# Two gates' weights and the second convolution product split anew in every chunk instead of reloaded from a scratch copy

## The chip, the cores and the metric

The kernel runs on one core of one Trainium2 chip. The metric is the device time of one execution in microseconds (us). Of the kernel before, three executions took 1346.3, 1350.51 and 1344.78 us, the median being 1346.3 us. A profile was taken of one further execution, of which all rows below are.

## What is computed

One layer over 2048 tokens of width 1024, with 16 learned meta tokens put ahead of them:

```
u = rms_norm(h, pre_norm_g)
glu_a, glu_b, conv_gate, q, k, v, sb_gate = split(u @ w_in)        # 7 x 512 columns
c = layer_norm(causal_depthwise_conv(glu_a * sigmoid(glu_b)))      # width 31
c = (silu(c) @ w_pw2 + b_pw2) * silu(conv_gate)
s = stick_breaking_attention(q, k, v) * silu(sb_gate)              # 8 heads of 64
h = h + rms_norm(concat(c, s) @ w_out, post_norm_g)
```

The attention is strictly causal; the weight of key s for query t is beta[t,s] times the product of (1 - beta) over the keys between them. Input and output are float32.

## The kernel before

**Chunks and streams.** The tokens are worked off in four chunks of 512 (`NCH`, `TC`). Chunk c has a main stream, `attention(c)`, and a fill stream, which is in this order the stick-breaking gate (`sb_gate`, weights `G_SG`), the output projection of chunk c-1 (`out_proj`, weights `w_out`), the convolution gate (`conv_gate`, weights `G_CG`), the second convolution product (`conv_out`, weights `w_pw2`) and the input projection of chunk c+1 (`in_proj`: GLU, keys, values, queries). Beside them run the convolution's taps (on DVE, or for some channel groups of chunks 2 and 3 on ACT and POOL as `conv_apart`), the layer norm of the convolution (`conv_norm`) and the split of its result into `mixs` (`conv_parts`). A small planner at build time (`Clock`, `Engine`, `merge`, `step`) keeps a model of each engine's time and writes all instructions out in one order; on the chip every engine then works its queue in that order, and an instruction that waits holds up all behind it. All instructions carry the line of the planner's `issue` helper, L206, so the rows are told apart by tile names.

**Products in three parts.** Each float32 operand is taken as a high part (rounded to float32r) and a low part (the rest), and each product is three matmuls: high by high, high by low, low by high. The two parts of a weight slab (128 partitions by 512 columns) come from `split` (line 442): ACT copies the slab into the high part, then POOL (DVE for seven early slabs) subtracts it from the slab and writes the low part.

**Where the weights come from.** `specs` (465) lists every use of every slab in order, with a turn: 0 for the input projection of chunk 0, and 1 + c for what chunk c's fill stream uses. There are 76 slabs: 56 of `w_in` (8 to each of the seven 512-column groups), 4 of `w_pw2`, 16 of `w_out`. A use goes one of two ways (`prepare`, 538):

- taken apart: two neighbouring slabs come in one 512 KB load from the input (`load_raw`, tile `wr`, named `wr<-wpack`), and `split` writes the parts into a `w` tile;
- kept: both parts, made earlier and stored by a DMA from POOL's queue (`keep_it`, `wscr<-w`, 512 KB a slab), come back with one 512 KB load a slab (`w<-wscr`, or `wr<-wscr`).

Turn 0 takes its slabs apart and stores nothing. From turn 1 on each slab is taken apart at its first use, stored, and kept from then on. So chunk 0's gates, `w_pw2` and the input projection of chunk 1 are taken apart and stored, chunk 1 still does that with `w_out`, and all else is kept.

**Slots.** There are four `w` tiles (`WB`) and two `wr` tiles (`RAWS`). While raw pairs are still to come the `wr` tiles hold them, two pairs ahead; once no raw pair is left they serve kept slabs as well, so that six slabs can be under way:

```
if tags.count("w") < WB:
    tag, bufs = "w", WB
elif not (raws or todo_raw) and tags.count("wr") < RAWS:
    tag, bufs = "wr", RAWS
```

A product gives a slot back (`release`, 580) after the last matmul of a slab; `out_proj` holds the four slabs of a column group through its first half and gives them back one by one in the second.

**Marks.** A string among an action's outputs is a mark; `force(mark)` (268) makes the planner write out, there and then, all pending actions that bear it. The values of a chunk are made by `values` (935) for four groups of two heads: differences, transposes on PE (`turn`), split, and a store to DRAM (`vscr<-mixs`). All four groups bear the mark `"v"`. `load_v` (1203) forces it ahead of the first loads of a chunk's own values (`vk<-vscr`); so do `meta_v`, `meta_keys` and `tail`.

Of the kernel before, what the change touches and what calls it, by code (L numbers as in the profile page):

```python
# [19 lines left out]
P = 128  # L20
# [3 lines left out]
NM = 16  # L24
# [230 lines left out]
def trunk(ctx: ExitStack, tc: tile.TileContext, x, xturn, meta, cpack, post_g, wpack, out):  # L255
# [16 lines left out]
    def when(what, ins, outs=(), engine=None, date=0.0, tag=None):  # L272
        soon.append(Later(clock, what, ins, outs, engine, date, tag))
# [191 lines left out]
    def specs():  # L465
        def cols(g):
            for j in range(NJ):
                yield w_in, (g + j) * P, P, 0, KD

        def proj_specs(c):  # L470
            for j in range(NJ):
                yield w_in, (G_B + j) * P, P, 0, KD
                yield w_in, (G_A + j) * P, P, 0, KD
            yield from cols(G_K)
            yield from cols(G_V)
            yield from cols(G_Q)

        def out_specs(k0, k1):
            for n in range(0, D, OC):
                yield w_out, n, OC, k0, k1  # L480

        def chunk(c):
            yield from cols(G_SG)
            if c > 0:
                yield from out_specs(0, KD)
            yield from cols(G_CG)
            for j in range(NJ):
                yield w_pw2, j * P, P, 0, NJ
            if c + 1 < NCH:
                yield from proj_specs(c + 1)  # L490
            else:

                for n in (*range(0, D, OC), *range(D // 2, D, OC)):
                    yield w_out, n, OC, 0, KD - 1

        for spec in proj_specs(0):
            yield 0, spec
        for c in range(NCH):
            for spec in chunk(c):
                yield 1 + c, spec  # L500
# [9 lines left out]
    place = {key: wscr[i] for i, key in enumerate(again)}  # L510
    order = []
    there = set()
    for turn, (w, n0, cols, ka, kb) in specs():
        step_k = 4 * P // cols
        for k0 in range(ka, kb, step_k):
            key = w, n0, cols, k0
            n = (min(k0 + step_k, kb) - k0) * cols
            kept, save = key in there, key not in there and key in place and turn > 0
            if save:
                there.add(key)  # L520
            order.append((key, n, kept, save))
# [413 lines left out]
    def values(c):  # L935

        for j in range(NJ):
            vts = []  # L940

            def ev_v(pt, o, n):
                if not vts:
                    vt = T("ev", [P, 1 + NM + TC], EV)
                    vts.append(vt)
                    if c == 0:
                        pool.memset(vt[:, 0:1], 0.0)
                    else:
                        pool.tensor_copy(
                            vt[:, NM : NM + 1], vcol[(c - 1) % 2][:, j, NTB - 1 :]  # L950
                        )
                act.activation(vts[0][:, 1 + o : 1 + o + n], pt, AF.Copy)

            yield from proj(c, G_V + j, ev_v, True)

            def differences(vt, j):
                o = 0 if c == 0 else NM
                dv = T("ev", [P, 1 + NM + TC], EV)[:, : NM + TC]
                pool.tensor_tensor(
                    dv[:, o:], vt[:, o : NM + TC], vt[:, o + 1 :], op=ALU.subtract  # L960
                )
                pool.tensor_copy(vcol[c % 2][:, j], vt[:, NM + P :: P])
                when(lambda: turn(dv, j, P, NM, NTB), [dv], ["v"], tag="T")
                if c == 0:
                    when(lambda: turn(dv, j, NM, 0, 1), [dv], ["v"], tag="T")

            def turn(dv, j, rows, t0, nb):
                pt = PT("T", [P, NTB, P])[:rows, :nb]
                for b in range(nb):
                    pe.transpose(pt[:, b], dv[:, t0 + b * rows : t0 + (b + 1) * rows], ident)  # L970
                for b in range(0, nb, 2):
                    n = min(2, nb - b)
                    part = T("mixs", [P, 2, 4, HD], 8, F32R)[:rows, 0:n]
                    hi, lo = part[:, :, 0::3, :], part[:, :, 1:3, :]
                    d = pt[:, b : b + n].rearrange("p b (h d) -> p b h d", d=HD)
                    act.activation(hi, d, AF.Copy)
                    dve.tensor_tensor(lo, d, hi.bitcast(F32), op=ALU.subtract)
                    row = c * TC + t0 + b * rows
                    when(
                        lambda row=row, n=n, part=part: sp.dma_start(  # L980
                            vscr[j, row : row + n * rows, :].rearrange(
                                "(b p) d -> p b d", p=rows
                            ),
                            part.rearrange("p b k d -> p b (k d)").bitcast(F32),
                        ),
                        [part], ["v"],
                    )

            when(lambda vt=vts[0], j=j: differences(vt, j), [vts[0]], [vcol[c % 2], "v"])
            if c == 0 and j == 0:  # L990
                in_us(4.5, meta_k, outs=[km])

# [8 lines left out]
                )  # L1001

    def meta_v():
        force("v")
        for h in range(NH):
            e, j = h % 2, h // 2
            rows = slice(e * HD, (e + 1) * HD)
            for i in range(2):
                blk = (0 if i == 0 else 1) if e == 0 else (3 if i == 0 else 2)
                sp.dma_start(  # L1010
                    vm[h * NM : (h + 1) * NM, i, j, rows].bitcast(F32),
                    vscr[j, 0:NM, blk * HD : (blk + 1) * HD],
                )
# [186 lines left out]
    def attention(c, mixs):  # L1200
        heads = {}

        def load_v(h, kc):
            if kc == c:
                force("v")
            s0, e = NM + kc * TC, h % 2
            vk = T("vk", [P, NTB, P], 2, F32R)
            sp.dma_start(
                vk.bitcast(F32),
                vscr[h // 2, s0 : s0 + TC, e * P : (e + 1) * P].rearrange(  # L1210
                    "(b p) d -> p b d", p=P
                ),
            )
            return vk
# [208 lines left out]
    def meta_keys(c, h0, h1, mixs):  # L1423
# [4 lines left out]
            given=lambda: all(("total", c, h) in keep for h in range(h1))  # L1428
            and (c < NCH - 1 or ("conv", c) in keep)
        )  # L1430
        force("v")
        bm = ev()[:, :TC].rearrange("p (b h s) -> p b h s", b=NTB, h=NH)
        hold.add(bm.name)
        if part:
# [339 lines left out]
    def tail(c):  # L1774


        force("v")
        sw, gates = [], [T("mixc", [P, TC], 8) for _ in range(NJ)]
        one = [conv_gate(c, gates), conv_out(c, sw, gates, mixc[c])]
        two = [conv_parts(c, accs[c], sw)]  # L1780
        if c + 1 < NCH:
            one.append(in_proj(c + 1))
            two.append(turn_in(c + 1))
        else:
            one.insert(1, last_room(c))
        yield from either(chain(*one), chain(*two))
# [117 lines left out]
```

## Time and profile before

| | |
|---|---|
| median of three executions | 1346.3 us |
| the profiled execution, its own time | 1350.2 us |
| its span | 1348.5 us |
| PE busy | 1315.5 us, 98% |
| DVE busy | 1014.4 us, 75% |
| ACT busy | 723.5 us, 54% |
| POOL busy | 644.6 us, 48% |
| moved by DMA | 304.96 MB, mean 226 GB/s |
| granted PE clock over the span | 0.994 |

PE is the tensor engine and PEld its weight load, DVE the vector, ACT the scalar and POOL the GpSimd engine; SPq is the queue of SyncE, which issues most DMAs. "mm<-uh,w" reads: tile `mm` was written from tiles `uh` and `w`. Busy time of PE counts the pipelined ends of matmuls, so 98% doesn't mean that nothing is left; idle time in a short stretch is what shows a stall. "[7.88 <-DMA wr<-wpack]" behind an instruction says that its engine stood idle 7.88 us before it, and that the landing of that DMA ended the wait.

By the evacuations and stores in the trace the stages lie thus, in us from the span's start: input projection 0 to about 133; chunk 0's gates and `conv_out` to 218; input projection of chunk 1 to about 355; chunk 1's gates, output projection and `conv_out` to 500; input projection of chunk 2 to 664; the same two of chunk 2 to 830 and 1013; chunk 3's to 1250; then the end.

### The profile page before, as it was taken

What the parts mean: (1) busy time and instruction counts of PE and PEld (TensorE: products, weight loads), DVE (VectorE), ACT (ScalarE), POOL (GpSimd) and SP (SyncE); (2) the same over time, 40 slices, a digit from 0 to 9 for tenths busy, and PEclk for the clock granted to TensorE, in tenths of its full rate; (3) what the DMA queues carried; (4) which work ended last, traced back from release to release, by engine and by line L of the source; (5) the groups of instructions that cost most, each with busy time, mean ns of one, the idle gap of its engine ahead of it and who ended that gap; (6) DMA issues with size and microseconds to landing.
All of it is one profiled execution on the core that took longest, in us unless ns stands there. A gap on an engine that the chain in (4) does not pass through costs nothing.

```text
span 1348.5 us, 21801 instructions
## 1 busy us (share of the span) xinstructions
PE 1315.5 (98%) x7582; PEld 1128.2 (84%) x7582; DVE 1014.4 (75%) x1426; ACT 723.5 (54%) x1443; POOL 644.6 (48%) x781
## 2 busy tenths in 40 slices
PE   8999989999999999999999999999999999999997
PEld 8997868887789877887789988888777899988797
DVE  5999875998985467984495478895548989798865
ACT  6443444344446453476644455478775656555542
POOL 3555567667456540487731243199885121141300
PEclk9999989999999999999999999999999999999999
DMA  6376975899977894686766596557677545687645
GB/s 225 131 213 217 311 261 209 274 328 307 352 236 255 286 341 134 203 239 210 263 214 189 186 326 210 165 181 228 212 218 250 160 143 154 186 278 216 200 156 180
DMA packets 163774, 304.96 MB, mean 226 GB/s; under 512 B 16704, under 2 KB 71168, under 8 KB 163664
## 3 DMA queue, kind: packets, MB, share of 16 engines
q1 hardware_dynamic: 149360, 253.49, 60.0%
q0 software_dynamic: 14304, 50.08, 9.5%
q8 instruction: 60, 0.98, 0.3%
q14 instruction: 50, 0.41, 0.1%
HBM read 221.85 MB, written 81.66 MB: 225 GB/s over the span
## 4 chain that ended last, share of the span: by engine, by line
PE 78%; DVE 8%; DMA 5%; ACT 4%; issue 3%; POOL 2%; SPq 1%; DVEq 0%; ACTq 0%; POOLq 0%
PE mm L206 50%; PE T L206 19%; PE av L206 8%; DMA tok<-x 2%; DVE tok L206 2%; DVE cv L206 1%; DVE pr L206 1%; ACT ev L206 1%; DVE al L206 1%; DMA wr<-wpack 1%; DMA ev<-x 1%; DVE ul L206 1%; DMA ev<-post_g 1%; POOL ev L206 1%; SPq L206 1%
## 5 line engine op out<-in xcount | busy, mean ns | idle before, releaser
L206 PE MATMUL mm<-uh,w 128*128 128x512 f32 (+1 forms) x1632 | 508.4, 372 | 0.4 <-ACT uh L206 0.4
L206 PEld LDWEIGHTS mm<-uh,w 128*128 128x128 f32 x1632 | 294.6, 189 | 48.7 <-ACT uh L206 0.8
L206 DVE TENSOR_TENSOR al<-T,ah 128x512 fp32r<-128x512 f32 (+3 forms) x323 | 194.0, 601 | 159.3 <-ACT ah L206 158.0
L206 PE MATMUL mm<-ul,w 128*128 128x512 f32 (+1 forms) x816 | 300.3, 368 | 1.1 <-DVE ul L206 1.1
L206 DVE TENSOR_TENSOR_SCAN pr<-T,pr,zcol 128x512 f32<-128x512 f32 x192 | 245.0, 1276 | 49.7 <-ACT T L206 44.5
L206 ACT ACTIVATE ah<-T 128x512 fp32r<-128x512 f32 (+3 forms) x323 | 171.7, 532 | 151.0 <-PE T L206 149.6
L206 DVE SCALAR_TENSOR_TENSOR cv<-ct,cp,cv 128x512 f32<-128x512 f32 x319 | 239.2, 750 | 7.1
L206 ACT ACTIVATE T<-T 128x512 f32<-128x512 f32 (+2 forms) x320 | 167.5, 525 | 107.2 <-PE T L206 100.6
L206 POOL TENSOR_TENSOR acc<-acc,pd 128x512 f32<-128x512 f32 x150 | 194.4, 1296 | 44.5 <-ACT pd L206 37.5
L206 PE MATMUL T<-kk,q 128*128 128x512 f32 (+2 forms) x640 | 195.4, 388 | 4.3 <-DVE ul L206 2.6
L206 POOL TENSOR_TENSOR w<-wr,w 128x512 fp32r<-128x512 f32 x109 | 141.0, 1295 | 91.1 <-ACT w L206 81.0
L206 PE MATMUL T<-ident,pr 128*128 128x128 f32 x1088 | 172.1, 273 | 1.6 <-DVE al L206 1.0
L206 PEld LDWEIGHTS mm<-ul,w 128*128 128x128 f32 x816 | 154.2, 189 | 21.7 <-DVE ul L206 1.5
L206 PEld LDWEIGHTS T<-ident,pr 128*128 128x128 f32 x1088 | 133.5, 140 | 33.6 <-DVE pr L206 2.4
L206 DVE TENSOR_TENSOR_SCAN pr<-T,tri 128x128 f32<-128x128 f32 (+3 forms) x128 | 103.9, 815 | 26.4 <-ACT T L206 25.6
L206 PEld LDWEIGHTS T<-kk,q 128*128 128x128 f32 x640 | 105.9, 190 | 20.4 <-DVE ul L206 3.8
L206 PE MATMUL av<-ah,vk 128*128 128x512 f32 (+1 forms) x320 | 117.3, 367 | 1.4 <-ACT ev L206 1.4
L206 ACT ACTIVATE w<-wr 128x512 fp32r<-128x512 f32 x116 | 72.6, 628 | 85.3 <-PE mm L206 39.9
L206 PE MATMUL av<-al,vk 128*128 128x512 f32 (+1 forms) x320 | 117.1, 366 | 0.0
L206 ACT ACTIVATE pd<-ct,cp 128x512 f32<-128x512 f32 x150 | 106.0, 717 | 19.0 <-POOL acc L206 18.1
L206 PE MATMUL mm<-uh,wr 128*128 128x512 f32 x320 | 115.0, 402 | 0.0
L206 POOL COPY cm<-pr 128x1 f32<-128x1 f32 x120 | 25.4, 213 | 139.0 <-DVE pr L206 137.7
(190 smaller groups left out, 1816.8 us busy)
## 6 DMA issues: line engine op xcount, KB each, us to landing
w<-wscr SPq DMA_DIRECT2D x128, 512.0 KB, 4.3
wscr<-w POOLq DMA_DIRECT2D x76, 512.0 KB, 5.5
wr<-wscr SPq DMA_DIRECT2D x62, 512.0 KB, 4.2
wr<-wpack SPq DMA_DIRECT2D x57, 512.0 KB, 5.3
kk<-kscr SPq DMA_DIRECT2D x80, 256.0 KB, 5.1
vk<-vscr SPq DMA_DIRECT2D x80, 256.0 KB, 4.0
q<-qscr SPq DMA_DIRECT2D x64, 256.0 KB, 5.7
tok<-x SPq DMA_DIRECT2D x16, 512.0 KB, 7.0
```

The costliest lines, as they stand in the source:

```text
L206: return call(out, *args, **kw)
```

## The change

Slabs of the two gates (`G_SG`, `G_CG`) and of `w_pw2` are never stored and never kept: they are taken apart in each of the four chunks. The other groups go as before. And each of the four groups of values has a mark of its own, `"v0"` to `"v3"`; `load_v` forces only the one of its head, while the other places force all four.

```diff
     order = []
     there = set()
+    apart = [g + j for g in (G_SG, G_CG) for j in range(NJ)]
     for turn, (w, n0, cols, ka, kb) in specs():
...
             kept, save = key in there, key not in there and key in place and turn > 0
+
+            save = save and (w == w_out or w == w_in and n0 // P not in apart)
             if save:
                 there.add(key)
...
-                when(lambda: turn(dv, j, P, NM, NTB), [dv], ["v"], tag="T")
+                when(lambda: turn(dv, j, P, NM, NTB), [dv], [f"v{j}"], tag="T")
...
-                        [part], ["v"],
+                        [part], [f"v{j}"],
...
-            when(lambda vt=vts[0], j=j: differences(vt, j), [vts[0]], [vcol[c % 2], "v"])
+            when(lambda vt=vts[0], j=j: differences(vt, j), [vts[0]], [vcol[c % 2], f"v{j}"])
...
         def load_v(h, kc):
             if kc == c:
-                force("v")
+                force(f"v{h // 2}")
...
     def tail(c):
-        force("v")
+        for j in range(NJ):
+            force(f"v{j}")
```

`meta_v` and `meta_keys` change as `tail` does.

## Rows read from the trace of the kernel before

**Rows 1.** The page's first part: busy time of each engine, share of the span, instructions.

```profile
PE 1315.5 (98%) x7582; PEld 1128.2 (84%) x7582; DVE 1014.4 (75%) x1426; ACT 723.5 (54%) x1443; POOL 644.6 (48%) x781
```

**Rows 2.** Stretches of the span that follow the stages: from and to, length, busy time (and instructions) of PE, PEld, DVE, ACT and POOL, granted PE clock, busy share of the DMA engines, GB/s.

```profile
126.00:230.00 104.00, 97.99 (x456) 79.35 (x455) 73.44 (x110) 46.35 (x91) 66.81 (x89) 0.93 0.76 263
230.00:345.00 115.00, 114.34 (x546) 93.20 (x546) 104.31 (x158) 50.27 (x102) 79.46 (x105) 1.00 0.92 309
...
455.00:500.00 45.00, 43.57 (x213) 35.73 (x212) 28.93 (x39) 22.13 (x47) 22.24 (x34) 1.00 0.93 343
...
780.00:830.00 50.00, 49.16 (x248) 40.07 (x247) 39.57 (x49) 25.10 (x50) 21.68 (x32) 1.00 0.91 307
...
1180.00:1250.00 70.00, 69.80 (x371) 57.84 (x370) 62.52 (x79) 40.14 (x80) 21.53 (x30) 1.00 0.77 243
```

**Rows 3.** The same view in steps of 5 us, in chunk 0.

```profile
170.00:175.00 5.00, 4.04 (x21) 3.05 (x20) 4.89 (x8) 0.00 (x0) 1.38 (x3) 1.00 1.03 408
175.00:180.00 5.00, 2.64 (x13) 2.27 (x14) 2.38 (x6) 2.50 (x5) 2.38 (x3) 0.72 0.49 186
180.00:185.00 5.00, 5.00 (x18) 4.12 (x17) 3.12 (x7) 0.00 (x0) 4.17 (x11) 0.59 0.69 250
...
195.00:200.00 5.00, 3.25 (x22) 2.70 (x21) 4.30 (x7) 3.62 (x8) 4.45 (x6) 1.00 1.00 360
200.00:205.00 5.00, 4.16 (x17) 3.09 (x16) 4.65 (x7) 3.96 (x9) 3.56 (x5) 0.61 0.76 256
205.00:210.00 5.00, 5.00 (x26) 4.19 (x25) 2.86 (x5) 2.29 (x4) 1.39 (x3) 0.70 0.03 12
```

**Rows 4.** The chain of waits that ended last, in chunk 0: start, duration, what.

```profile
165.62 10.86 DMA wr<-wpack
```

**Rows 5.** The timeline at the same place, of ACT, DVE and PE: start, duration, instruction, and idle time before it with what ended it.

```profile
176.58 0.63 ACT L206 ACTIVATE w<-wr 128x512 fp32r<-128x512 f32 x1 [7.88 <-DMA wr<-wpack]
177.12 0.58 ACT L206 ACTIVATE ah<-T 128x512 fp32r<-128x512 f32 x1
...
174.41 0.75 DVE L206 SCALAR_TENSOR_TENSOR acc<-ct,cp,cv 128x512 f32<-128x512 f32 x1
177.73 0.69 DVE L206 TENSOR_TENSOR al<-T,ah 128x512 fp32r<-128x512 f32 x1 [2.58 <-ACT ah L206]
...
178.48 1.12 PE L206 MATMUL T<-ident,acc 128*128 128x128 f32 x4 [2.15 <-DVE al L206]
```

**Rows 6.** DMA of the stretch 126 to 203: queues (packets, MB, share of the 16 engines), and two of the issues with their count, size and median us to landing.

```profile
q1 hardware_dynamic: 8138, 12.16, 51.1%
q0 software_dynamic: 2826, 10.27, 33.4%
...
wscr<-w POOLq DMA_DIRECT2D x20, 512.0 KB, 6.4
wr<-wpack SPq DMA_DIRECT2D x10, 512.0 KB, 7.2
```

**Rows 7.** What ACT waited for in 126 to 230 (total us, times, longest), first row, and in 203 to 1250, one row.

```profile
ACT w L206 <- DMA wr<-wpack: 19.7, 4, 7.9
...
ACT w L206 <- DMA wr<-wpack: 1.6, 1, 1.6
```

**Rows 8.** POOL's timeline where PE stands the second time.

```profile
197.10 0.57 POOL L206 DMA_DIRECT2D wscr<-w  x1
...
199.44 1.29 POOL L206 TENSOR_TENSOR mixs<-acc,mixs 128x512 fp32r<-128x512 f32 x1
200.67 0.56 POOL L206 DMA_DIRECT2D wscr<-w  x1
```

**Rows 9.** Groups of the whole span, shapes kept apart: busy us, mean ns of one, idle before.

```profile
L206 POOL TENSOR_TENSOR w<-wr,w 128x512 fp32r<-128x512 f32 x109 | 141.0, 1295 | 91.1 <-ACT w L206 81.0 <-PE T L206 8.2 <-DMA w<-wscr 1.5
L206 ACT ACTIVATE w<-wr 128x512 fp32r<-128x512 f32 x116 | 72.6, 628 | 85.3 <-PE mm L206 39.9 <-DMA wr<-wpack 23.1 <-POOL cm L206 8.1
L206 POOL DMA_DIRECT2D wscr<-w x76 | 43.3, 570 | 14.1 <-POOL w L206 10.4 <-POOL cm L206 2.2 <-PE T L206 0.6
```

**Rows 10.** The output projection in chunk 2, 710 to 780: ACT's evacuations of its eight half groups (first and last start), and the loads of kept slabs there (count, size, median us to landing); last, the landing of all DMAs of tile `w` over the span.

```profile
L206 ACT ACTIVATE tok<-mm x8: 597/599/601, 717.2 to 778.8; 128x512 f32<-128x512 f32 x8
...
w<-wscr SPq DMA_DIRECT2D x10, 512.0 KB, 4.5
...
DMA to landing us min/median/max: 2.9/4.7/10.5
```

**Rows 11.** Stores and loads of the values around two chunk beginnings, 90 to 140 and 305 to 366: count, durations of the issue, first and last start.

```profile
L206 SPq DMA_DIRECT2D vscr<-mixs x12: 359/387/477, 91.6 to 113.4; - x12
L206 SPq DMA_DIRECT2D vk<-vscr x1: 1064/1064/1064, 138.4 to 138.4; - x1
...
L206 SPq DMA_DIRECT2D vscr<-mixs x8: 359/366/709, 309.6 to 332.3; - x8
```

**Rows 12.** DVE's residual add over the span (durations min/median/max), and DVE and POOL at one of the long ones.

```profile
L206 DVE SCALAR_TENSOR_TENSOR tok<-tok,st,ev x24: 715/735/4282, 462.5 to 1210.3; 128x512 f32<-128x512 f32 x24
...
458.64 5.09 POOL L206 TENSOR_TENSOR mixs<-acc,mixs 128x512 fp32r<-128x512 f32 x4
462.51 3.02 DVE L206 SCALAR_TENSOR_TENSOR tok<-tok,st,ev 128x512 f32<-128x512 f32 x1 [2.62 <-POOL mixs L206]
463.70 1.28 POOL L206 TENSOR_TENSOR tok<-tok,ev 128x512 f32<-128x512 f32 x1
```

More of the change, by code (lines that the diff above doesn't have):

```diff
@@ L962, in differences @@
                 pool.tensor_copy(vcol[c % 2][:, j], vt[:, NM + P :: P])
-                when(lambda: turn(dv, j, P, NM, NTB), [dv], ["v"], tag="T")
+                when(lambda: turn(dv, j, P, NM, NTB), [dv], [f"v{j}"], tag="T")
                 if c == 0:
-                    when(lambda: turn(dv, j, NM, 0, 1), [dv], ["v"], tag="T")
+                    when(lambda: turn(dv, j, NM, 0, 1), [dv], [f"v{j}"], tag="T")
             def turn(dv, j, rows, t0, nb):
@@ L1430, in meta_keys @@
         )
-        force("v")
+        for j in range(NJ):
+            force(f"v{j}")
         bm = ev()[:, :TC].rearrange("p (b h s) -> p b h s", b=NTB, h=NH)
@@ L1774, in tail @@
     def tail(c):
-        force("v")
+        for j in range(NJ):
+            force(f"v{j}")
         sw, gates = [], [T("mixc", [P, TC], 8) for _ in range(NJ)]
```

## The prediction

> **What bounds the kernel now.** I read the busy table first: PE is busy for 98% of the span [rows 1], so only a stall of PE, or a stretch in which it runs slow, can give time back. The stretches by stage come next, and in them I look for PE's idle time (length less busy) and its granted clock. From 230 on PE stands 0.66 us in 115, 1.43 in 45, 0.84 in 50 and 0.20 in 70, always at the full clock of 2.4 GHz; in 126 to 230 it stands 104.00 - 97.99 = 6.01 us and the clock is 0.93 [rows 2]. That is chunk 0, where the gates and `w_pw2` are taken apart and stored. In steps of 5 us there are two dips. The first: 0.96 + 2.36 = 3.32 us idle in 170 to 180, and behind it a clock of 0.72 and 0.59 for 175 to 185, so that PE runs part of this time at its lower level, 1.2 GHz. The second: 1.75 + 0.84 = 2.59 us idle in 195 to 205, clock 0.61 and 0.70 for 200 to 210 [rows 3].
>
> The chain of waits names the first dip's cause: a load of two raw slabs, issued at 165.62, that took 10.86 us [rows 4]. The timeline shows how it reaches PE. ACT stood idle 7.88 us before the high part of that slab; the attention's `ah` was queued behind it, DVE's `al` waited for `ah`, and PE waited 2.15 us for `al` [rows 5]. Of DMA time in 126 to 203, the queue that carries the stores takes 33.4% of the engines' span of 84.9% in all; the 20 stores land after 6.4 us and the raw loads after 7.2 us, in the median [rows 6].
>
> **The change part by part.** The sum is made against the profiled execution, 1350.2 us of its own time (span 1348.5 and 1.7 around it); it lay 3.9 us above the median of 1346.3 and may show these dips larger than a usual execution does.
>
> *Stores that go.* Eight slabs of `G_SG`, eight of `G_CG` and four of `w_pw2` are no longer stored: 20 DMA issues on POOL of 0.570 us [rows 9], 11.4 us of POOL's time, and 10.5 MB, nearly all between 126 and 218. With them goes up to 33.4 of 84.9 parts of the DMA engines' load [rows 6], so the raw loads of this stretch, whose waits cost ACT 19.7 us in four stalls [rows 7], should land early enough for the first dip to vanish. It costs 3.32 us idle and, at the lower clock, (0.28 + 0.41) x 5 = 3.45 us [rows 3]; of the slow time a part falls on idle time, at most the 2.36 us of 175 to 180, so that up to 1.2 us is counted twice; I take off half of that. Gain 6.2 us; bounds 0 and 6.8.
>
> *The second dip.* Here PE waits on the way to `conv_out` and to the transposes of the next chunk's input. POOL splits `mixs` there, and two stores stand in its queue among these splits, 0.57 and 0.56 us [rows 8]; with the 14.1 / 76 = 0.19 us that POOL stands before each store [rows 9] this is 1.5 us of that way. Bounds: nothing, or the whole dip, 2.59 idle plus (0.39 + 0.30) x 5 = 3.45 us, 6.0 us [rows 3]. The nearest row is the queue itself: I take 1.5.
>
> *Splits that come.* In chunks 1, 2 and 3 twenty slabs each are taken apart once more: 60 times 0.628 us on ACT and 1.295 us on POOL [rows 9], 37.7 and 77.7 us. They lie in the gate stages, where in 455 to 500, 780 to 830 and 1180 to 1250 POOL is busy 22, 22 and 22 us of 45, 50 and 70 and ACT 22, 25 and 40 [rows 2]: beside PE. What it can cost is that the attention's evacuations stand behind a split. For the price there is a stage that does just this: 230 to 345 takes 40 slabs apart and stores them too, at a DMA share of 0.92, and PE stands 0.66 us [rows 2]; from 203 to 1250, with 56 splits, ACT waits for raw loads 1.6 us in all [rows 7]. By that row 60 splits cost 1.0 us; by the first dip, one for each of three chunks, 18.6 us. I take 1.5, near the row with forty of them.
>
> *Loads that change.* 60 kept loads of 512 KB become 30 raw ones of the same size. These bytes lie beside PE's work; less traffic could take at most the 1.43 us in 455 to 500 [rows 2]. I take nothing.
>
> *Two slots fewer.* Raw pairs now come until chunk 3's `w_pw2`, so the two `wr` tiles hold no kept slabs until then and four slabs are under way in place of six. SP's queue takes the raw loads too, and a raw load that waits for its tile would hold up key, value and query loads behind it; the planner issues it when it thinks the tile free. The tightest place is the output projection: halves are 61.6 / 7 = 8.8 us apart, slabs come free one by one in the second half, so the next group's first slab has three quarters of that, 6.6 us, to land, and loads take 4.5 [rows 10]. That is enough by 2.1 us. The longest landing of tile `w` is 10.5 us [rows 10]: if each of three group boundaries in chunks 2 and 3 met that, 6 x 3.9 = 23 us. I take 1.0.
>
> *Marks.* A chunk's stores of values have all been issued well before the first own load: 113.4 against 138.4 in chunk 0, and 332.3 for chunk 1, whose gates by the stages begin some 20 us later [rows 11]. There is nothing pending to force, so one mark or four write out the same order: 0, both ways.
>
> Sum: -6.2 - 1.5 + 1.5 + 1.0 = -5.2 us. On the profiled execution that is 1345.0 us, on the median 1341.1 us, 0.4% less. About 0.5%, 6.7 us, is what a measurement of this kernel can tell from no change: faster starts below 1339.6 us, slower above 1353.0.
>
> **A forecast's rivals.**
>
> *Nothing comes back.* The first dip goes, but the second grows by as much, since `conv_out` hangs on DVE's taps, which end at 174.41 + 0.75 = 175.2 [rows 5] whatever the weights do. For: PE's gate work would then run out some 6 us sooner. Against: the norm's transposes of that sum themselves stood in PE's queue until 178.48 [rows 5], and what follows ran at the lower clock, so the chain should come forward with the rest. Time: 1346.3 + 1.5 + 1.0 - 1.5 = 1347.3 us.
>
> *Both dips go.* Without the stores POOL and the DMA engines are early enough for PE to stand too briefly for the clock to fall at all in the second dip. For: its idle time is only 2.59 us [rows 3]. Against: its waits are for DVE and ACT in a chain with little slack. Time: 1346.3 - 6.2 - 6.0 + 2.5 = 1336.6 us.
>
> *Slower: ACT behind a late raw load, now in three more chunks.* In the gate stages of chunks 1 to 3 the DMA engines are busy too, 0.93, 0.91 and 0.77 [rows 2]. Where a kept slab that is late holds up only the matmul that reads it, a raw slab that is late holds up ACT, and with it the attention. It decides when a pair takes longer to land than its predecessor to be used, as the 10.86 us of the first dip [rows 4]. For: the same stages, the same queue. Against: each chunk's first two pairs of a gate are loaded long ahead, and the stages lose half of their weight bytes. Price: one dip of 6.2 us in each, 18.6, less the 1.5 already counted: 1341.1 + 17.1 = 1358.2 us.
>
> *Slower: DVE held by POOL.* The residual add reads two SBUF tiles. Of 24 the median is 0.735 us, but the first of a chunk takes up to 4.282; at 462.51 it lasted 3.02 us, until POOL's run of four `mixs` splits and one more product was over [rows 12]. New splits of `G_CG` come just there. If the four of the slots that are free prolong that run in each of three chunks, DVE stands 3 x 4 x 1.295 = 15.5 us more, and if all of it reached PE the time is 1341.1 + 15.5 = 1356.6 us. Against: in 455 to 500, with such an add, PE stood only 1.43 us [rows 2], and splits come one by one as slots are given back. The Trainium skill, page "SBUF — State Buffer", section "Who interferes with whom", has the rule: a DVE instruction with two SBUF inputs contends with a GpSimd instruction that reads SBUF, and the one that comes second is blocked entirely, while one with a PSUM input is free. By that rule the 60 new subtractions, which read two SBUF tiles, are just what such adds wait for; the trace agrees, with the 3.02 us beside the median of 0.735.
>
> **How the numbers follow.** The forecast has 0.46, its own range being 1337 to 1345, with two fifths of it below 1339.6. Nothing comes back 0.14; both dips go 0.22; late raw loads 0.12; DVE held 0.06, a third of it within the bound. Faster: 0.18 + 0.22 = 0.40. Within 0.5%: 0.28 + 0.14 + 0.02 = 0.44. Slower: 0.12 + 0.04 = 0.16. The range goes down to 1331, below both dips gone with nothing paid for slots and splits, and up to 1355, where it takes in two late raw loads of three.
>
> **What would show it.** Right: ACT's waits for raw loads in 126 to 230 fall from 19.7 us to under 6; PE's idle time in chunk 0 falls by some 3 us, with one stretch at the lower clock in place of two; splits on ACT rise from 116 to 176, stores fall from 76 to 56; in 455 to 500, 780 to 830 and 1180 to 1250 PE's idle time stays within 2 us of what it was. Wrong: a new dip of PE in one of those stages, with ACT idle before `w<-wr` (late raw load) or a residual add of over 4 us before it (DVE held); PE idle at the output projection of chunk 2 behind a load of `w` (slots); or the first dip still there although no store runs beside it, which would mean that the raw load was late for another reason, such as the small reads of `vm` or the queue of SP.

## The result, and the profile after

The changed kernel takes 1353.67 us (median of nine executions, 1352.3 to 1355.27); the kernel before took 1346.3 us in nine beside them. The ratio is 1.005, with a 95% interval of 1.0034 to 1.0066: slower by some 6.7 us by the ratio (7.4 by the two medians), where 1341.1 was forecast. The time lies inside the stated range of 1331 to 1355, but on the other side of the kernel before. The profiled execution took 1353.9 us, its span 1351.9.

The busy table answers to [rows 1]: PE has the same work, ACT and POOL have the sixty splits more, and DVE, which got no new instruction, is busy for 10.6 us longer in the same 1426 instructions.

```profile
PE 1312.0 (97%) x7582; PEld 1124.4 (83%) x7582; DVE 1025.0 (76%) x1426; ACT 754.0 (56%) x1503; POOL 712.8 (53%) x821
```

The stretches of the changed kernel by stage, columns as in [rows 2], and a last one for everything from 230 to 1300:

```profile
126.00:230.00 104.00, 100.47 (x496) 82.05 (x496) 80.35 (x121) 49.43 (x97) 61.15 (x76) 1.00 0.60 186
230.00:345.00 115.00, 114.34 (x546) 92.80 (x545) 105.19 (x160) 50.63 (x102) 77.16 (x102) 1.00 0.93 310
...
455.00:500.00 45.00, 41.77 (x204) 33.59 (x203) 34.17 (x40) 25.09 (x48) 33.67 (x40) 1.00 0.88 282
...
780.00:830.00 50.00, 48.79 (x252) 40.34 (x251) 41.48 (x51) 29.35 (x57) 33.38 (x40) 1.00 0.74 250
...
1180.00:1250.00 70.00, 67.94 (x355) 55.67 (x354) 64.16 (x76) 42.00 (x83) 31.69 (x38) 1.00 0.63 201
230.00:1300.00 1070.00, 1053.35 (x5917) 891.58 (x5916) 815.21 (x1097) 628.87 (x1247) 586.30 (x662) 1.00 0.68 213
```

The same view of a further execution of the kernel before (1345.37 us), with two steps of 5 us at the place of the first dip:

```profile
126.00:230.00 104.00, 99.71 (x477) 80.95 (x476) 76.83 (x116) 47.62 (x94) 70.36 (x94) 0.97 0.81 275
230.00:1300.00 1070.00, 1058.47 (x5961) 898.67 (x5960) 809.62 (x1106) 601.37 (x1192) 510.00 (x604) 1.00 0.71 229
...
170.00:175.00 5.00, 4.13 (x22) 3.13 (x20) 4.86 (x9) 0.00 (x0) 1.46 (x3) 1.00 1.04 409
175.00:180.00 5.00, 4.19 (x26) 3.58 (x27) 3.99 (x9) 2.50 (x5) 3.75 (x5) 1.00 0.75 286
```

Three things are to be read. Chunk 0 got the relief: the clock is 1.00 in 126 to 230 and the DMA share fell from 0.76 to 0.60. From 230 to 1300 PE stands 1070 - 1053.35 = 16.65 us, against 11.53 in the other execution of the kernel before. And the first dip of [rows 3] is hardly there in that execution: 0.87 + 0.81 us idle at the full clock, in place of 3.32 us and a slow stretch.

The clock of 1.00 is that of one execution. The run `e9_late20` below has every instruction of chunk 0 in the same order, and there PE still runs slow behind the second dip:

```profile
195.00:200.00 5.00, 4.85 (x23) 3.93 (x23) 4.49 (x7) 3.10 (x8) 3.28 (x4) 0.66 0.26 97
```

The raw loads behaved as forecast. ACT's wait for them in 126 to 230, answering to [rows 7]:

```profile
ACT w L206 <- DMA wr<-wpack: 1.7, 1, 1.7
```

and the DMA of 126 to 203, answering to [rows 6]:

```profile
q0 software_dynamic: 48, 0.13, 0.4%
...
wr<-wpack SPq DMA_DIRECT2D x10, 512.0 KB, 3.5
```

The wait fell from 19.7 to 1.7 us (to 7.0 in the execution of `e9_late20`), the landing from 7.2 to 3.5.

The last part of the time is behind the last piece of work. In the chain the last instruction of DVE ends at 1343.67, yet the span is 1351.9; in the kernel before the two are 1345.07 and 1348.5. What lies between is seen at the line that closes the program (durations min/median/max in ns, first and last start), first of the kernel before:

```profile
L1900 POOLq DRAIN  x3: 40/102/2014, 1342.5 to 1348.2; - x3
```

and of the changed one:

```profile
L1906 POOLq DRAIN  x3: 40/93/10097, 1341.1 to 1351.7; - x3
```

POOL's queue ends with an instruction that took 2.0 us and now takes 10.1, so that it ends 7.5 us after DVE's last work. No part of the prediction had it.

### The profile page after: what moved, and what is told of

Read it like the earlier page. It is cut to its first block, busy times and chain, and to the rows that moved or that the text cites. A ratio compares the mean times of both kernels' runs of the same rounds, so it can differ in the third digit from the quotient of the medians.

```text
span 1351.9 us, 21858 instructions
## 1 busy us (share of the span) xinstructions
PE 1312.0 (97%) x7582; PEld 1124.4 (83%) x7582; DVE 1025.0 (76%) x1426; ACT 754.0 (56%) x1503; POOL 712.8 (53%) x821
## 4 chain that ended last, share of the span: by engine, by line
PE 75%; DVE 10%; DMA 3%; ACT 3%; issue 3%; POOL 3%; SPq 1%; DVEq 0%; POOLq 0%; ACTq 0%
PE mm L206 47%; PE T L206 19%; PE av L206 8%; DVE cv L206 3%; DVE tok L206 2%; DVE pr L206 2%; POOL w L206 1%; DVE al L206 1%; ACT ev L206 1%; DMA tok<-x 1%; DMA wr<-wpack 1%; POOL ev L206 1%; DVE ul L206 1%; SPq L206 1%; ACT uh L206 1%
## 5 line engine op out<-in xcount | busy, mean ns | idle before, releaser
L206 PE MATMUL mm<-uh,w 128*128 128x512 f32 (+1 forms) x1952 | 623.1, 377 | 1.7 <-ACT uh L206 1.6
L206 PEld LDWEIGHTS mm<-uh,w 128*128 128x128 f32 x1952 | 354.8, 189 | 61.9 <-ACT uh L206 1.9
L206 PE MATMUL mm<-ul,w 128*128 128x512 f32 (+1 forms) x976 | 363.5, 372 | 0.7 <-DVE ul L206 0.7
L206 POOL TENSOR_TENSOR w<-wr,w 128x512 fp32r<-128x512 f32 x169 | 221.9, 1316 | 116.4 <-ACT w L206 111.5
L206 PEld LDWEIGHTS mm<-ul,w 128*128 128x128 f32 x976 | 184.5, 189 | 26.8 <-DVE ul L206 1.3
L206 ACT ACTIVATE w<-wr 128x512 fp32r<-128x512 f32 x176 | 110.1, 628 | 95.0 <-PE mm L206 56.4
L206 PE MATMUL mm<-w,mixc 128*128 128x256 f32 x648 | 87.6, 284 | 0.2 <-ACT tok L206 0.2
```

What stands on the lines that cost most here:

```text
L206: return call(out, *args, **kw)
```

## The experiments

All ratios are to the kernel before, executed beside each run on the same chip. Behind each stands its 95% interval. The diffs show the lines that do the work; lines that only pick out the slabs are left out.

**The two parts of the change, each alone, and the kernel before once more.** `e1_marks` has the four marks and stores and reloads as before; `e2_apart` is the weights' part with one mark:

```diff
-                        [part], ["v"],
+                        [part], [f"v{j}"],
```

```diff
+            save = save and (w == w_out or w == w_in and n0 // P not in apart)
```

> The kernel before with the marks alone taken from the change; weights as before, 130 DMAs on POOL's queue. In the changed kernel's trace the last visible work ends 1.4 us earlier than before, and the span is 3.4 us longer, because POOL's last DRAIN lasts 10.1 us instead of 2.0. Theory 'drain': that drain hangs on what POOL's DMA queue did (110 DMAs instead of 130), so here it lasts 2 us and the time is within 3 us of before. Rival 'splits': the slowdown comes from the weights' splits in chunks 1 to 3, and the drain is an accident of the profile; then here too the time is within 3 us of before, but the drain may have either length. By the prediction's step on the marks the time is exactly that of before; against it, a load of a chunk's own values also lies in the middle of the chunk, beside the next chunk's values, so the order does change there, for which I expect 0 to -3 us.

> The kernel before with the weights' part of the change alone, one mark for all values; 110 DMAs on POOL's queue. Theory 'drain': the last DRAIN lasts 10 us and the time is 1351 to 1356 us. Rival 'splits': the same time, with PE's idle time in the gate stages of chunks 1 to 3 several us above that of before, whatever the drain does. Rival 'marks': the marks are what cost; then 1346 or below.

> The kernel before once more, one look. Its nine runs lie at 1344 to 1347 us and, three of them with the profiled one, at 1350. Theory: at 1344 to 1347 one or both of the stretches in which PE runs at its lower clock in chunk 0 (177 to 184 and 201 to 208 us in the profile read) are missing, about 3.4 us each, and the gain that the prediction counted from the first dip is smaller in a usual run. Rival: both stretches are there and the difference lies at the end of the program.

Measured: marks 1343.65 us, 0.9987 (0.9972 to 1.0001); weights 1355.28 us, 1.0071 (1.0049 to 1.0092). The loss is the weights' part; the marks give about 1.7 us, or nothing. POOL's last drain took 2.012 us with the marks alone and 10.099 with the weights' part alone. Of the two dips in chunk 0 the further execution of the kernel before (`e4_before_again`, 1345.37 us) has only the second: its clock is 0.70 and 0.62 in 195 to 205 and 1.00 in 170 to 190.

That the marks change the order at all is seen in SP's queue. The kernel before again, stores of the next chunk's values and loads of this chunk's:

```profile
612.19 5.83 SPq L206 DMA_DIRECT2D vscr<-mixs  x3
618.11 0.45 SPq L206 DMA_DIRECT2D vk<-vscr  x1
```

and with marks alone:

```profile
611.50 0.39 SPq L206 DMA_DIRECT2D vscr<-mixs  x1
612.63 0.37 SPq L206 DMA_DIRECT2D vk<-vscr  x1
615.82 1.24 SPq L206 DMA_DIRECT2D vscr<-mixs  x2
```

A load for chunk 1's own attention waited behind three stores of chunk 2's values, forced out by the mark that both chunks share. Near that place PE stood for 1.65 us in the kernel before, and for 0.21 with marks:

```profile
615.23 0.44 PE L206 MATMUL T<-ident,ev 128*128 128x128 f32 x2 [1.65 <-POOL ev L206]
```

It waited for POOL's `ev` there, and not for the load, which was issued only at 618.11. How the order of the forced work delays `ev` wasn't followed.

**The stores of chunk 0, put back.** The changed kernel, with the twenty slabs stored in chunk 0 as before and never read:

```diff
             save = save and (w == w_out or w == w_in and n0 // P not in apart)
+            save = save or (key in place and turn == 1)
```

> The changed kernel, but the 20 slabs of the gates and of the second convolution product are stored in chunk 0 as before (and never read back): 130 DMAs on POOL's queue, 60 splits more than before. Theory 'drain': the last DRAIN is back at 2 us; the end comes about 5 us earlier by that, while the first dip of PE in chunk 0 (6.2 us by the prediction) may come back, so 1346 to 1355 us, and the drain tells. Rival 'splits': drain of any length, and a time not below that of the changed kernel.

Measured: 1351.83 us, 1.0038 (1.002 to 1.0056), with POOL's last drain at 2.012 us. In chunk 0 PE stands 6.32 us of 126 to 230 (3.53 in the changed kernel), with two slow stretches, as in the kernel before. Against `e1_marks`, which ran beside it on the same chip and differs from it in the sixty splits, their loads and the slots alone, it is longer by 0.0051, 6.9 us with an uncertainty of 3. To price the stores alone, it has to be held against the run below that has the short drain without the stores, 1.0021: the stores themselves cost 0.0017, 2.3 us, with an uncertainty of 3.

**What sets the last drain.** The stores that went were DMAs of POOL's queue: 130 of them before (76 stores of slabs, 30 and 24 others), 110 after. Small ones were added to the changed kernel, in chunk 0 (`e7_tiny`) or just before the last piece of work (20, and in `e11` 10, in `e12` 40):

```diff
+        for key in (bits * 2)[:20]:
+            pool.dma_start(place[key][:1, 0, :4], ident[:1, :4])
         out_last(parts[0], *mixs[-1][NJ - 1])
```

> The changed kernel with 20 more DMAs on POOL's queue in chunk 0, at the places of the stores that went, of 32 bytes each (one partition, two pieces of four values) in place of 512 KB; nothing reads them. If POOL's last drain goes by the number of DMAs that its queue issued, it is 2.0 us with 130 of them, and the time falls by about 5 us to 1348 to 1349. If it goes by the bytes or the packets that the queue moved, it stays at 10.1 us and the time at 1353 to 1354.

> The changed kernel with 20 DMAs of 16 bytes more on POOL's queue just before the last piece of work, where POOL is idle for 47 us (some 1285 to 1331); everything before stays as it was. If the last drain goes by the number of DMAs on POOL's queue, it is 2.0 us again and the span loses about 5 us, with the same idle time of PE (16.6 us behind 230): 1346.3 + 6.7 - 5 = about 1348 us. If small DMAs just before the end lengthen the drain, or if it depends on where the DMAs lie, it stays at 10 us or more and the time at 1353.

> As e9_late20 with 10 small DMAs, 120 on POOL's queue in all. It shows where between 110 (10.1 us) and 130 (2.0 us) the drain changes: 2.0, 10.1 or a value between, 6 us if it goes evenly with the number.

> As e9_late20 with 40 small DMAs, 150 in all. If the drain only shrinks with the number, it is 2.0 us or less; if the number matters by its remainder in some round of the queue, it may be long again, up to 10 us.

With 20 late ones, 10 and 40, the line at the program's end reads:

```profile
L1909 POOLq DRAIN  x3: 40/93/1851, 1342.0 to 1347.6; - x3
```

```profile
L1909 POOLq DRAIN  x3: 40/102/10922, 1341.1 to 1352.5; - x3
```

```profile
L1909 POOLq DRAIN  x3: 40/102/3490, 1340.1 to 1345.7; - x3
```

| DMAs on POOL's queue | 110 | 120 | 130 (large stores) | 130 (small, early or late) | 150 |
|---|---|---|---|---|---|
| longest drain, us | 10.10 | 10.92 | 2.01 | 1.85 | 3.49 |

So neither bytes nor place matter much, but the number does, and not by a plain more or less: in these runs the drain rises by 0.08 us for each DMA, from 110 to 120 as from 130 to 150, and falls by 9 us somewhere between 120 and 130. `e9_late20` took 1348.04 us, 1.0021 (1.0004 to 1.0038): 3.9 us less than the changed kernel, as expected, with the same idle time of PE behind 230. `e7_tiny` missed by its ratio: its drain is short too, but it took 1350.34 us, 1.0048 (1.0033 to 1.0062). There the twenty issues stand in POOL's queue in chunk 0, where POOL is busy for 71.8 us of 126 to 230 in place of 61.2. That they take back what the drain gives is not shown: PE stands no longer in that stretch (3.15 us, against 3.53), and the profiled execution, 1350.47 us, is 3.4 below that of the changed kernel. Runs `e11` and `e12` were executed once each (1354.69 and 1347.88 us).

**Which half of a split costs.** ACT's half done twice, in the 60 splits of chunks 1 to 3; then POOL's half made by DVE in those (with the 20 late DMAs):

```diff
-            act.activation(hi, y, AF.Copy)
+            for _ in range(n):
+                act.activation(hi, y, AF.Copy)
```

```diff
-                    dve if len(todo_w) in FIRST else pool,
+                    dve if len(todo_w) in FIRST or len(order) - len(todo_w) in twice else pool,
```

> The changed kernel with ACT's half of each of the 60 new splits in chunks 1 to 3 done twice (60 times 0.63 us more on ACT, nothing more on POOL, the result unchanged). If the splits cost time because the attention's work stands behind them in ACT's queue, the loss in those chunks about doubles: 1353.7 + 6 = about 1360 us. If it is POOL's half (its queue, or DVE held by it), ACT's extra 38 us lie beside PE and the time stays within 2 us of 1353.7.

> As e9_late20, and in addition the low part of the 60 new splits of chunks 1 to 3 is made by DVE in place of POOL. If POOL's half is what costs time there (its own queue, or DVE held by it), PE's idle time behind 230 falls from 16.6 us towards the 11.5 of the kernel before, and the time by some 4 us against e9_late20. If it is the load of work as such, or the loads, DVE's further 42 us cost as much or more and the time stays or rises.

Measured: `e8_act2` 1352.0 us, 1.0059 (1.0035 to 1.0083), no different from the change itself: 35 us more of ACT lie beside PE. `e10_dvelow` 1343.31 us, 0.9974 (0.9955 to 0.9992): 6.3 us less than `e9_late20` by the ratio, 4.7 by the medians, each of its twelve executions below each of the other's, and faster than both kernels. POOL's half is what costs. Two reservations: the planner laid out the order anew for it, so a part of the gain can be the order's, and DVE's further splits may have taken a part back. The stretch from 230 to 1300, of `e9_late20`:

```profile
230.00:1300.00 1070.00, 1053.41 (x5912) 891.32 (x5911) 814.96 (x1096) 628.06 (x1246) 597.38 (x682) 1.00 0.67 213
```

and of `e10_dvelow`:

```profile
230.00:1300.00 1070.00, 1056.51 (x5949) 895.22 (x5948) 852.40 (x1162) 630.55 (x1250) 527.28 (x622) 1.00 0.67 213
```

POOL is 70 us less busy, DVE 37 more, and PE stands 13.49 us in place of 16.59.

Late raw loads are not what `e10_dvelow` got rid of: in 230 to 1250 ACT waits for them 10.5 us there, as in the changed kernel (10.6). Nor does a raw tile come free much sooner: SP's queue, which reloads it, waits in 230 to 1300 for POOL's splits 137.3 us in `e9_late20`, and for POOL's and DVE's together 57.9 + 68.8 = 126.7 in `e10_dvelow`.

**How POOL's half costs: its queue, or DVE held.** In the changed kernel the 24 residual adds of [rows 12] take longer. Their group in the kernel before again (busy us, mean ns, idle before):

```profile
L206 DVE SCALAR_TENSOR_TENSOR tok<-tok,st,ev 128x512 f32<-128x512 f32 x24 | 22.4, 941 | 7.5 <-DMA ev<-x 7.5
```

and in the changed one:

```profile
L206 DVE SCALAR_TENSOR_TENSOR tok<-tok,st,ev 128x512 f32<-128x512 f32 x24 | 30.7, 1289 | 2.7 <-DMA ev<-x 2.7
```

DVE's timeline there in chunk 1's gates:

```profile
466.99 2.84 DVE L206 SCALAR_TENSOR_TENSOR tok<-tok,st,ev 128x512 f32<-128x512 f32 x2
...
474.33 1.53 DVE L206 SCALAR_TENSOR_TENSOR tok<-tok,st,ev 128x512 f32<-128x512 f32 x1
...
476.99 0.72 DVE L206 SCALAR_TENSOR_TENSOR tok<-tok,st,ev 128x512 f32<-128x512 f32 x1
```

POOL at the same time:

```profile
465.26 2.54 POOL L206 TENSOR_TENSOR w<-wr,w 128x512 fp32r<-128x512 f32 x2
...
472.77 2.54 POOL L206 TENSOR_TENSOR w<-wr,w 128x512 fp32r<-128x512 f32 x2 [0.54 <-ACT w L206]
```

The add of 474.33 begins beside POOL's second split, which ends at 475.31, and lasts until 475.86; the next, at 476.99 and with no split beside it, takes 0.72.

Which of DVE's other instructions grew tells the same. Multiplications of two tiles in SBUF (the on-chip memory that holds most tiles), first in the kernel before (again its further execution), then in the changed one:

```profile
L206 DVE TENSOR_TENSOR tok<-tok 128x512 f32<-128x512 f32 x12 | 10.5, 879 | 0.4
...
L206 DVE TENSOR_TENSOR tok<-tok 128x512 f32<-128x512 f32 x12 | 14.0, 1166 | 0.4
```

and subtractions of which one input, `T`, lies in PSUM (where PE writes its results), in the same order:

```profile
L206 DVE TENSOR_TENSOR al<-T,ah 128x512 fp32r<-128x512 f32 x227 | 154.1, 679 | 109.2 <-ACT ah L206 108.3
...
L206 DVE TENSOR_TENSOR al<-T,ah 128x512 fp32r<-128x512 f32 x227 | 154.2, 679 | 103.4 <-ACT ah L206 102.5
```

The first have grown by a third, the second not at all. In `e10_dvelow` the multiplications are back at 826 ns. The convolution's taps, whose running sum `cv` lies in PSUM, aren't held either. These are their times (min/median/max) in 230 to 345 of the kernel before, the stage of many splits from which the prediction took its price:

```profile
L206 DVE SCALAR_TENSOR_TENSOR cv<-ct,cp,cv x94: 727/756/757, 234.7 to 344.9; 128x512 f32<-128x512 f32 x94
```

To tell the hold from a fuller queue, POOL got the same load back in the order of `e10_dvelow`, once as fills of a dead tile (one that nothing reads any more), which read nothing, and once as the subtraction into that tile, which reads two; and both again with the planner counting the time (`e13` the first, `e14` the second, `e15` and `e16` the same with the third):

```diff
+                for n in (512, 512, 128):
+                    nc.gpsimd.memset(row[:, :n], 0.0)
```

```diff
+                nc.gpsimd.tensor_tensor(row[:, :512], y, hi.bitcast(F32), op=ALU.subtract)
```

```diff
+                pool.now = max(pool.now, clock.at(hi)) + 1.25
```

> The kernel of e10_dvelow with every instruction in the same order, and beside each of the 60 splits that DVE makes there three fills of a dead tile on POOL (512, 512 and 128 columns, about 1.26 us by the fills of the kernel before, as long as the subtraction that went): POOL's queue is as full as in e9_late20, but POOL reads nothing there. If POOL's own queue is what the splits burdened, PE's idle time behind 230 goes back from 13.5 towards 16.6 us and the time from 1343.3 to about 1347; if POOL's reads hold DVE, both stay where e10_dvelow had them, with residual adds at a median near 0.74 us.

> The same, but with the subtraction itself on POOL, of the same slab and its high part, into the dead tile in place of the fills: as long, but it reads two tiles of SBUF. If POOL's reads hold DVE, the residual adds grow again (24 of them took 30.9 us in the changed kernel, 21.2 in e10_dvelow) and the time goes to 1347 or above, DVE having its own 42 us of splits as well; if it is POOL's queue, this and the run with fills take the same time.

> As e13_poolset (fills of a dead tile on POOL beside each split that DVE makes), but the planner counts 1.25 us of POOL for each and lays out the order by it, as it did for the real subtractions. The loss of 13.8 us in e13_poolset may be that of an order that knew nothing of POOL's load. If a planned load of POOL's queue is free, the time goes back to 1343 to 1345 us; if POOL's queue costs even when planned, it is 1347 or more.

> The same order to the instruction, with the subtraction on POOL in place of the fills. What this takes more than e15_planset is what POOL's reads cost by holding DVE (its residual adds and its own splits): some 5 to 10 us by e14_poolsub against e13_poolset if that theory holds, 0 if not.

| | time, us | ratio | PE idle 230 to 1300 | 24 adds, us | DVE's 67 splits, us |
|---|---|---|---|---|---|
| `e10_dvelow`, neither | 1343.31 | 0.9974 (0.9955 to 0.9992) | 13.49 | 20.9 | 59.6 |
| `e13`, fills | 1357.1 | 1.0079 (1.0061 to 1.0097) | 23.10 | 20.2 | 58.4 |
| `e14`, subtraction | 1367.01 | 1.0148 (1.0129 to 1.0167) | 30.05 | 27.4 | 70.0 |
| `e15`, fills planned | 1358.13 | 1.01 (1.0082 to 1.0118) | 21.36 | 20.8 | 57.6 |
| `e16`, subtraction planned | 1363.53 | 1.0142 (1.0121 to 1.0163) | 25.99 | 25.9 | 67.1 |

The rows for the adds, with fills and with the subtraction, in one order:

```profile
L206 DVE SCALAR_TENSOR_TENSOR tok<-tok,st,ev 128x512 f32<-128x512 f32 x24 | 20.2, 855 | 0.4 <-DMA ev<-x 0.3
```

```profile
L206 DVE SCALAR_TENSOR_TENSOR tok<-tok,st,ev 128x512 f32<-128x512 f32 x24 | 27.4, 1156 | 0.7 <-DMA ev<-x 0.6
```

Neither theory stands alone. Reads of POOL hold DVE: between two kernels of one order DVE's adds and splits grow by 18.8 us (`e14` against `e13`) and 14.6 us (`e16` against `e15`), and the times by 0.0069 and 0.0042, some 9 and 6 us. Not all of that time need come through DVE. The added subtraction also reads the raw tile, and SP's next load into that tile waits for it; in `e14`, 230 to 1300:

```profile
SPq L206 <- POOL row L452: 21.4, 9, 5.2
```

How much of the 9 and 6 us goes this way isn't shown. A fuller queue costs as well, even when planned: the fills alone take 14 to 17 us, and DVE's rows don't move. These runs have DVE's own splits on top, so that their sizes can't be carried over to the change; how its 6.3 us divide between hold and queue stays open, as does through which of POOL's products the queue reaches PE.

**Stores in a later chunk.** The apart groups stored in chunk 2 or in chunk 1 and reloaded from then on, which brings back 130 DMAs and saves 20 or 40 splits (`e5_turn3`, and `e6_turn2` with `turn >= 2`):

```diff
-            save = save and (w == w_out or w == w_in and n0 // P not in apart)
+            save = save and (w == w_out or w == w_in and n0 // P not in apart or turn >= 3)
```

> The changed kernel, but the two gates' slabs and those of the second convolution product are stored in chunk 2 and reloaded in chunk 3, so that they are taken apart anew in chunks 1 and 2 only; POOL issues 130 DMAs as before, and chunk 0 stores nothing of them. If the time lost is the extra splits of chunks 1 to 3 (some 6 us by the milestones, of them 3.5 in chunk 3) and POOL's last drain (some 5 us), both are partly undone: drain 2.0 us, 1353.7 - 5 - 3 = about 1345 us. If the drain is set by where the stores lie and not by how many there are, it stays at 10.1 us and the time at 1350. If the loss in chunk 3 comes from the marks' other order, the time is about 1348.

> The same with the store in chunk 1 and reloads in chunks 2 and 3: splits anew in chunk 1 alone, 130 DMAs on POOL. Theory (chunk 0 relieved by 3 us, splits cost some 2 us a chunk, drain 2.0 us, marks -1.7 us): 1346.3 - 3 - 1.7 + 2 = about 1343.5 us, faster than both kernels. Rival, that 20 stores of 512 KB disturb any gate stage in which they stand by as much as they did chunk 0: 1346 to 1349 us.

Both missed: 1350.76 us, 1.0045 (1.0027 to 1.0063), and 1356.27 us, 1.0096 (1.0079 to 1.0113), although their drains are 2.0 us. The loss is in the stage behind the stores. Of `e6_turn2`, chunk 1's `conv_out` to the end of the input projection, 486 to 572:

```profile
486.00:572.00 86.00, 76.32 (x365) 60.97 (x366) 68.58 (x96) 37.43 (x74) 23.83 (x37) 0.98 0.67 215
```

SP's queue there, and below it what SP waited for in 455 to 520 (us, times, longest):

```profile
491.62 7.30 SPq L206 DMA_DIRECT2D w<-wscr  x3
499.24 0.37 SPq L206 DMA_DIRECT2D vk<-vscr  x1
499.66 1.72 SPq L206 DMA_DIRECT2D q<-qscr  x2
```

```profile
SPq L206 <- POOL w L206: 22.9, 5, 5.8
...
SPq L206 <- DMA wscr<-w: 6.0, 2, 5.0
```

PE stands 9.7 us in this stretch. Where raw slabs give way to kept ones, SP's queue waits for POOL's splits (22.9 us; 11.8 in the changed kernel) and for stores to land, and the loads of the attention's values, queries and keys stand behind the loads of kept slabs. It is the keys that PE waits for, twice, 5.4 of its 9.7 us in 486 to 572:

```profile
PE T L206 <- DMA kk<-kscr: 5.4, 2, 3.0
```

`e5_turn3` loses time in chunk 2, where PE is busy for 85.34 of 90 us in 806 to 896, but not by the same wait: PE waits there for DVE's `pr` (3.0 us, four times) more than for a load of keys (0.6 us), and what delays `pr` wasn't followed. So in `e6_turn2` a store has a price where it stands and another where its slab is first reloaded, and the expectations had only the first.

## Why the prediction was wrong

By ratios, each difference uncertain by 2 to 3.5 us: stores of chunk 0 gone -2.3 us (`e9` against `e3`), marks -1.7 (`e1`), POOL's half of the splits +6.3 (`e9` against `e10`), the last drain +3.9 (the change against `e9`). Sum +6.2; measured +6.7. That the sum closes says less than it seems: the last two terms are by themselves the whole way from `e10` to the change, so all that is tested is that `e10` lies 3.5 us below the kernel before, where the stores and the marks give 4.0. The splits have a second price, 6.9 us, by `e3` against `e1`. That the time fell inside the stated range was luck: its upper end stood for late raw loads, and they came in `e10` too, which is faster than the kernel before. Step by step:

- **Stores that go, -6.2: right in kind, mis-sized.** ACT's wait, the landing and the clock did what was forecast. But the 6.2 us were read off one execution of 1350.2 us, 3.9 above the median, which the text itself noted; in another one PE stands 1.68 us in 170 to 180 at the full clock, although ACT waits 18.0 us for raw loads there too. With the second dip the gain is 2.3 us, not 7.7. Some of what chunk 0 gains is also taken back later: with the stores put back, PE stands 1070 - 1057.53 = 12.47 us from 230 to 1300, without them 16.59.
- **Second dip, -1.5: not shown.** PE still stands 2.13 + 1.30 + 0.10 = 3.5 us in 190 to 205. The fall of the clock behind it is gone in the profiled execution of the change, but there in that of `e9`, which has the same chunk 0.
- **Splits that come, +1.5: the step that failed.** They cost 6.3 us (`e9` against `e10`) or 6.9 (`e3` against `e1`). The price came from the stage of 230 to 345, which stands 0.66 us [rows 2] and takes forty slabs apart by the text (35 by the trace). That stage has no residual adds: the first of the 24 begins at 455.9 in the changed kernel. What DVE does there instead are mostly the convolution's taps, none of which is held. The row had the splits, but not the work that they meet. The one way to a cost that the text named, the attention's evacuations behind a split in ACT's queue, takes nothing that can be told (`e8`); the cost came by POOL's half, which it put beside PE at nothing.
- **DVE held by POOL, the rival with a chance of 0.06: the mechanism is there.** It priced 15.5 us more on DVE; the residual adds grew by 30.7 - 22.4 = 8.3. PE's idle time from 230 to 1300 grew by 5.1, but that is no measure of the hold: with the stores put back it is only 0.9 above the kernel before, although the splits are all there and the adds take 27.5 us. Its objection, that PE stood only 1.43 us in 455 to 500 with such an add, told of a stage that had no splits. The rule of the Trainium skill, page "SBUF — State Buffer", section "Who interferes with whom", was quoted beside it. It also says that a GpSimd instruction which only writes doesn't contend. By both halves of it the traces agree: the adds have a mean of 855 ns with fills and 1156 with subtractions.
- **Slots, +1.0: nothing.** In 710 to 780, chunk 2's output projection, PE is busy for all of 70.00 us, and in 1070 to 1180, chunk 3's, for all of 110.00.
- **Marks, 0 both ways: wrong in its reason.** The text looked at the start of a chunk, where nothing is pending. But `load_v` forces at every head's first own load, all through the chunk, and the shared mark then forces the next chunk's values. The gain, 1.7 us at best, is within what can be told from nothing.
- **The end: a term that was missing.** POOL's queue was counted for time (11.4 us) and for bytes, not for the number of its DMAs.
- **The signs: too coarse.** PE's idle time in the three gate stages stayed within 2 us of what it was, which was to show that the forecast is right: 3.23 against 1.43 in 455 to 500, 1.21 against 0.84 in 780 to 830, 2.06 against 0.20 in 1180 to 1250. Together that is 4.0 us. No residual add lasted over 4 us, the sign of the hold; the longest took 3.278, and it is their median that moved, from 0.735 to 1.138.

Late raw loads did come (ACT waits for them in 230 to 1250 seven times, 10.6 us, against 1.6 and, in the further execution of the kernel before, 5.1), but `e10_dvelow` has them too and is faster than the kernel before.

## What to carry to other kernels

A row that prices new work must come from a stage in which the same neighbours run: ask which instructions of the other engines will lie beside it, not only whether the stage was full. Ask also where the neighbours' inputs lie: here the held ones read two tiles of SBUF. Before pricing a dip, see it in a second execution, and before calling it gone as well. And look at what stands between the last instruction and the end of the span: here a change far from it moved it by 5 us.

## What the runs showed of the hardware that was not expected

The instruction that ends POOL's queue takes 1.85 to 10.92 us, by the number of DMAs that the queue has issued in the whole program: in these runs 0.08 us for each, with a fall of 9 us between 120 and 130. If the fall takes back one full round, the round would be some 9.9 / 0.082 = 120 DMAs (an estimate from 110, 120, 130 and 150; no run went through a second fall). Twenty DMAs of 16 bytes in a stretch where POOL is idle, which nothing reads, made the program 3.9 us faster by ratio, with an uncertainty of 3, and 4.1 us between the two profiled executions.

DVE's instructions with two inputs in SBUF took longer beside POOL's subtractions of two SBUF tiles (residual adds 1289 ns in place of 941, multiplications 1166 in place of 879, in the mean), and subtractions with one input in PSUM didn't (679 in both kernels). In the order of `e10_dvelow` the adds took 855 beside POOL's fills and 1156 beside its subtractions.
